# Gate and up pairs with seven products over ten of sixteen k tiles, and tokens kept in DRAM during a half step

## The chip, the cores and the metric

The kernel runs on one core of a Trainium2 chip. The metric is the device time of one execution in microseconds; for comparisons it is the median of several runs. A core has these engines: TensorE (PE in the profile; PEld is its loading of stationary operands), VectorE (DVE), ScalarE (ACT), GpSimd (POOL) and SyncE (SP), and 16 DMA engines. Each engine works through its own instructions in order and waits on semaphores for the others. SP and ACT issue plain DMAs here, POOL also DMAs that add to their destination (accumulating DMAs).

## The reference

A decoder layer over 256 tokens of width 2048, everything in float32. Two half steps, a SwiGLU block each, stand around a mixer and a cross-attention:

```
x = x + 0.5 * swiglu(rms_norm(x, ffn1_norm), ffn1_w_gate, ffn1_w_up, ffn1_w_down)
x = x + hybrid_mixer(rms_norm(x, mix_norm), ...)
x = x + cross_attention(rms_norm(x, xattn_norm), rms_norm(mem, mem_norm), ...)
x = x + 0.5 * swiglu(rms_norm(x, ffn2_norm), ffn2_w_gate, ffn2_w_up, ffn2_w_down)

def swiglu(h, w_gate, w_up, w_down):
    return (jax.nn.silu(h @ w_gate) * (h @ w_up)) @ w_down
```

The hidden width of a half step is 5632, so gate and up are 2048 x 5632 each and down is 5632 x 2048. The mixer and the cross-attention lie between the half steps and are called the middle stage here.

## The kernel before, in words

*Numbers.* A product is taken in a two-part split: each float32 operand is a rounded part "h" and the rest "l" (wh, wl for weights; xTh, xTl and hTh, hTl for tokens and hidden values), and three matmuls, h·h, l·h and h·l, make one product. `wsplit` (line 163, its instructions are `split`, line 160-161) makes wh with a copy on ACT (a "cast") and wl with a subtraction on DVE (a "sub") that reads the raw weights and wh.

*Tiling.* A k tile is 128 rows of a weight matrix; a weight group is 4 k tiles x 512 columns, 1 MB, loaded by one DMA that SP issues (`load`, line 150) into a raw tile. There are 16 k tiles over the model width, and eleven column tiles f over the hidden width. Tokens are two tiles t of 128. A matmul has 512 columns.

*Half step* (`ffn`, line 404). The column tiles are taken in three parts, (0..3), (4..7), (8..10). In a part each f takes a gate/up pair: gate and up products of the tokens, silu of gate (sg, ACT) times up (h, DVE), and a transposition of h (`turn`, lines 408-417) two items later. Then the part's hidden tiles are multiplied by down, in two Strassen groups of two output columns c each; what comes out is added into the tokens `xs` (line 469, DVE), which are kept in SBUF. After the last part `after` makes the next norm, or stores the output.

*Strassen groups* (`strassen`, line 240). The pair of weight columns (left, right) and two k groups (a, b) make seven products instead of eight. This document names them by TensorE's order: P1 (x from the left a weights, ral), P2 (y), P3 (x), P4 (the left b weights, rbl), P5 (x), P6 (the right b weights, rbr), and P7. For P2 and P3 the raw tile ral is added to in place on DVE (lines 255, 273 and 279), each time after the split before has read it; for P5 and P7 accumulating DMAs on POOL's queue add rbr to rar and rbl to ral (line 259). The sums of tokens that P2, P3, P5 and P6 need are made once in a half step (`sums_of`, line 215), and once in a part for h, among P6 of the part's last pair (`mid`); the first is kept in DRAM meanwhile. The k groups that are not in a and b are done plainly (`whole`, line 196), 24 matmuls each, left then right: L0, then P7, then R0, L1, R1. Down's part of three has only L0 and R0. The first pair of a half step is made without seven products (`plain_pair`, line 318).

So in a pair TensorE's order of items is P1 to P6, L0, P7, R0, L1, R1. The transposition of the h of the pair before stands between P2 and P3.

*Slots.* wh and wl have three buffers each (FWB = 3), taken in turn by all items: the split of an item can begin when the item three places ahead has released its slot. Raw tiles have six places in a half step (WRAW + FRAW), taken from a list in a fixed turn (`places`). `in_turn` (line 123) keeps loads, casts and subs each in the order of the program. Otherwise a scheduler orders the instructions of each engine by priority when the program is built; WPRI moves weights' work ahead of the rest.

## Time and profile before

| | |
|---|---|
| median of 3 runs | 1901.0 us (1900.52 to 1901.95) |
| profiled execution | 1900.82 us, span 1898.8 us |
| granted TensorE clock, mean | 0.998 |
| TensorE busy | 1885.3 us, 8616 matmuls |
| DVE, ACT, POOL busy | 1460.8, 1082.2, 123.0 us |
| DMA | 453.90 MB, mean 239 GB/s |

The span goes from the first to the last instruction of one execution. Busy time is the time in which an engine has an instruction under way; matmuls overlap, so that the time from one start to the next is shorter than a matmul's own. In a line of groups stand source line, engine, operation, output and inputs with shapes, the count, busy time in us and mean ns of one, and behind the second bar the idle time of the engine ahead of these instructions, with what ended it. In a timeline stand start and length in us, and in brackets the idle time ahead with its releaser. In a view by stretches stand the stretch, its length, busy time and count for PE, PEld, DVE, ACT and POOL, the granted clock (1.00 is full), the DMA engines' share and GB/s. In the list of DMAs the last number is the median time in us from issue to landing.

### The profile page before, as it was taken

To read this page: it belongs to the slowest core of one execution; us is meant where nothing else is said; L and a number is where in the kernel's file an instruction comes from. 1 tells how busy PE (TensorE), PEld (TensorE's weight loads), DVE (VectorE), ACT (ScalarE), POOL (GpSimd) and SP (SyncE) were. 2 spreads that over 40 slices of the span, in tenths; PEclk is the share of its full clock that TensorE was granted. 3 is DMA by queue.
4 is the path that set the end of the run, shared out by engine and by line. 5 is a ranking of instruction groups with operands and counts; after the bars stand their busy time and mean duration, and the time that the engine had idled before them with its cause. 6 is when DMAs were issued, how large, how long until landed. Compare 5 with 4: busy or idle time off the path is not lost.

```text
span 1898.8 us, 21625 instructions
## 1 busy us (share of the span) xinstructions
PE 1885.3 (99%) x8616; PEld 1561.7 (82%) x8616; DVE 1460.8 (77%) x1174; ACT 1082.2 (57%) x1043; POOL 123.0 (6%) x137
## 2 busy tenths in 40 slices
PE   9999999999999999999999999999999999999998
PEld 7788888888888878778888889888888888888887
DVE  7779887798888975446785565877888878887897
ACT  6556655555555656444576545555655556556663
POOL 2000000000000000002221000000000000000000
PEclk9999999999999999999999999999999999999999
DMA  9876787777777755445465554677768777787775
GB/s 371 294 241 225 244 305 277 274 249 245 269 243 269 260 167 184 157 167 193 170 230 205 190 191 155 245 253 277 232 233 288 262 266 277 256 281 233 241 252 191
DMA packets 68336, 453.90 MB, mean 239 GB/s; under 512 B 7659, under 2 KB 8811, under 8 KB 14860
## 3 DMA queue, kind: packets, MB, share of 16 engines
q1 hardware_dynamic: 56140, 370.74, 49.9%
q0 software_dynamic: 10944, 79.70, 18.7%
q10 hardware_dynamic: 1152, 2.10, 0.3%
q8 instruction: 67, 1.10, 0.2%
q14 instruction: 33, 0.27, 0.0%
HBM read 379.10 MB, written 6.29 MB: 203 GB/s over the span
## 4 chain that ended last, share of the span: by engine, by line
PE 95%; DVE 2%; ACT 1%; issue 1%; DMA 0%; SPq 0%; ACTq 0%; DVEq 0%
PE acc L201 25%; PE x L236 17%; PE acc L193 9%; PE acc L194 9%; PE acc L192 9%; PE acc L236 9%; PE x L201 9%; PE y L236 4%; DVE wl L161 1%; ACT wh L161 1%; PE tp L413 1%; DVE raw L255 1%; DMA raw<-in_ffn_w_up_dram 0%; PE tp L373 0%; PE dsp L690 0%
## 5 line engine op out<-in xcount | busy, mean ns | idle before, releaser
L161 DVE TENSOR_TENSOR wl<-raw,wh 128x2048 fp32r<-128x2048 f32 (+2 forms) x538 | 1014.6, 1905 | 351.8 <-ACT wh L161 351.0
L161 ACT CAST wh<-raw 128x2048 fp32r<-128x2048 f32 (+2 forms) x538 | 853.2, 1600 | 601.3 <-DVE raw L255 180.5
L192 PE MATMUL acc<-wh,xTh 128*128 128x512 f32 x544 | 214.7, 397 | 0.9 <-ACT wh L161 0.8
L193 PE MATMUL acc<-wl,xTh 128*128 128x512 f32 x544 | 212.8, 391 | 0.5 <-DVE wl L161 0.3
L194 PE MATMUL acc<-wh,xTl 128*128 128x512 f32 x544 | 212.5, 391 | 0.0
L255 DVE TENSOR_TENSOR raw<-raw 128x2048 f32<-128x2048 f32 x64 | 146.6, 2291 | 1.9
L259 POOL DMA_DIRECT2D raw<-raw x64 | 55.1, 861 | 1170.4 <-ACT sg L453 478.9
L201 PE MATMUL acc<-wh,xTh 128*128 128x512 f32 x480 | 121.8, 389 | 0.0
L201 PE MATMUL acc<-wl,xTh 128*128 128x512 f32 x480 | 121.8, 389 | 0.0
L201 PE MATMUL acc<-wh,xTl 128*128 128x512 f32 x480 | 121.8, 389 | 0.0
L193 PEld LDWEIGHTS acc<-wl,xTh 128*128 128x128 f32 x544 | 102.6, 189 | 22.9 <-DVE wl L161 2.1
L192 PEld LDWEIGHTS acc<-wh,xTh 128*128 128x128 f32 x544 | 102.4, 189 | 23.0 <-ACT wh L161 1.4
L194 PEld LDWEIGHTS acc<-wh,xTl 128*128 128x128 f32 x544 | 102.5, 188 | 21.5
L201 PEld LDWEIGHTS acc<-wh,xTl 128*128 128x128 f32 x480 | 90.1, 188 | 18.7
L201 PEld LDWEIGHTS acc<-wh,xTh 128*128 128x128 f32 x480 | 90.1, 188 | 18.7
L201 PEld LDWEIGHTS acc<-wl,xTh 128*128 128x128 f32 x480 | 90.1, 188 | 18.7
L236 PE MATMUL x<-wh,sh 128*128 128x512 f32 x256 | 71.8, 403 | 3.1 <-ACT wh L161 3.1
L236 PE MATMUL x<-wh,sl 128*128 128x512 f32 x256 | 69.5, 393 | 0.0
L236 PE MATMUL x<-wl,sh 128*128 128x512 f32 x256 | 69.2, 392 | 0.0
L453 ACT ACTIVATE sg<-acc,r 128x512 f32<-128x512 f32 x24 | 16.5, 690 | 90.1 <-PE acc L201 88.4
L201 PE MATMUL acc<-wl,hTh 128*128 128x512 f32 x232 | 59.3, 390 | 1.8 <-DVE wl L161 1.8
L201 PE MATMUL acc<-wh,hTh 128*128 128x512 f32 x232 | 59.0, 390 | 1.2 <-ACT wh L161 1.2
(339 smaller groups left out, 2827.0 us busy)
## 6 DMA issues: line engine op xcount, KB each, us to landing
raw<-in_ffn_w_down_dram SPq DMA_DIRECT2D x88, 1024.0 KB, 7.5
raw<-in_ffn_w_up_dram SPq DMA_DIRECT2D x87, 1024.0 KB, 8.8
raw<-in_ffn_w_gate_dram SPq DMA_DIRECT2D x86, 1024.0 KB, 8.7
raw<-raw POOLq DMA_DIRECT2D x64, 1024.0 KB, 6.9
raw<-in_w_in_dram SPq DMA_DIRECT2D x48, 1024.0 KB, 4.8
raw<-in_w_out_dram SPq DMA_DIRECT2D x16, 1024.0 KB, 4.8
sl<-ffn_sl POOLq DMA_DIRECT2D x4, 1024.0 KB, 9.0
sh<-ffn_sh POOLq DMA_DIRECT2D x4, 1024.0 KB, 13.0
```

Source lines behind the costliest of these rows:

```text
L161: return SC.copy(wh, src), V.tensor_sub(wl, src, wh.bitcast(F32))
L192: PE.matmul(acc[t], lh, wh, start=first and i == 0, stop=False, skip_group_check=seeded)
L193: PE.matmul(acc[t], lh, wl, start=False, stop=False, skip_group_check=seeded)
L194: PE.matmul(acc[t], ll, wh, start=False, stop=last and i == len(half) - 1, skip_group_check=seeded)
L201: PE.matmul(acc[t], lhs(w[0], t)[i], w[1 + j], start=False, stop=last and j == 1 and n == len(group) - 1, skip_group_check=True)
L236: PE.matmul(acc, lhs(k)[i], w[:, k], start=first, stop=j == 1 and k == 3, skip_group_check=not start)
L255: V.tensor_add(dst, x, y)
L259: G.dma_start(dst, x, accum_op=ALU.add)
L413: PE.transpose(tp[:, j], hs[t][:, j * P:(j + 1) * P], ident)
L453: SC.activation(s, gate[t], AF.Silu, scale=r[:, t:t + 1])
```

## The change: what it does

In a gate/up pair after the first, the seven products now take ten of the sixteen k tiles: a is the k tiles (8, 9, 10, 11, 6), b is (12, 13, 14, 15, 7), five each. The rest is plain: (0, 1, 2, 3) as L0 and R0, 24 matmuls each, and (4, 5) as L1 and R1, 12 each. A product of the pair has 15 matmuls instead of 12. Down's groups stay as they are, with four k tiles.

The tiles wh, wl and raw get room for five k tiles (WK), the raw places of a half step become five (FRAW = 2) and wh and wl keep three buffers. A five-tile load is two DMAs, a five-tile accumulation too (four tiles and one). The sums of tokens get a fifth tile (`more` in `sums_of`), with instructions of their own.

To make room, tokens leave SBUF during a half step: they lie in DRAM tiles `xd`. After the first two parts, what comes out of down is halved by ACT into y (`SC.activation`, four per group) and added to DRAM by an accumulating DMA; in the last part the tokens are loaded into `xc` and added to by DVE as before. At the end of the first half step two of the four token tiles go back to DRAM until the output projection, where SP loads them again; the other two stay. Buffers move between pools: h tiles are six instead of eight, with the fourth hidden tile of a part, the sums' scratch and `xc` in a pool `cp` of two buffers, and the middle stage has 41 instead of 44 small buffers. The stores of the kept sums, and for the first half step a copy of x to DRAM, are issued after the second pair of a half step.

```diff
-UB = 44
+UB = 41
-FRAW = 3
+FRAW = 2
+WK = 5
 FWB = 3
+SEVEN = ((8, 9, 10, 11, 6), (12, 13, 14, 15, 7))
+PLAIN = ((0, 1, 2, 3), (4, 5))
...
+    def CT(shape, dt, name):
+        return cp.tile(shape, dt, tag="c", name=name)
...
+    def wtile(tag, m, n=512):
+        half = phase["half_step"]
+        w = FT(tag, FWB if half else WB, [P, WK if half else 2, 512], F32R, tag)
+        return w.rearrange("p k n -> p (k n)")[:, :m * n].rearrange("p (k n) -> p k n", n=n)
...
-            in_turn("load", SY.dma_start(raw, W[c, g]))
+            raw = raw_tile(place, len(ks), n)
+            kn = W.shape[-2]
+            d = 0
+            while d < len(ks):
+                g, k = divmod(ks[d], kn)
+                m = sum(j // kn == g for j in ks[d:])
+                in_turn("load", SY.dma_start(raw[:, d:d + m], W[c, g, :, k:k + m]))
+                d += m
...
-    def sums_of(ga, gb):
+    def sums_of(ga, gb, more=None):
...
+        if more:
+            f5 = W2([P, 2, S], "f5")
+            V.tensor_add(f5, *(x.bitcast(F32) for x in more))
+            fs.append([f5[:, i:i + 1] for i in range(2)])
...
-                G.dma_start(dst, x, accum_op=ALU.add)
+                for ks in (slice(0, 4), slice(4, len(a))):
+                    if ks.start < len(a):
+                        G.dma_start(dst[:, ks], x[:, ks], accum_op=ALU.add)
...
-                    gate, upv = strassen(wg, f, wu, f, lhs_x, (2, 3), sums, (0, 1),
+                    gate, upv = strassen(wg, f, wu, f, lhs_x, SEVEN, sums, PLAIN,
                                          mid=sums_h if f == part[-1] else None)
...
             for c in range(0, NC, 2):
+                xc = {}
+                if end:
+                    for d in (c, c + 1):
+                        xc[d] = CT([P, TT, 512], F32, "xc")
+                        G.dma_start(xc[d], xd[d])
...
                 for d, acc in zip((c, c + 1), accs):
                     for t in range(TT):
-                        V.scalar_tensor_tensor(xs[d][:, t], acc[t], 0.5, xs[d][:, t], op0=ALU.mult, op1=ALU.add)
+                        if end:
+                            V.scalar_tensor_tensor(xc[d][:, t], acc[t], 0.5, xc[d][:, t], op0=ALU.mult, op1=ALU.add)
+                        else:
+                            with tc.high_priority(WPRI):
+                                y = W2([P, 512], "y")
+                                SC.activation(y, acc[t], AF.Copy, scale=0.5)
+                            G.dma_start(xd[d][:, t], y, accum_op=ALU.add)
...
+    for c in range(2):
+        xs[c] = FT("x", 2, [P, TT, 512], F32, "xs")
+        SY.dma_start(xs[c], xd[c])
...
             norm_chunk(d, xs[d], 64, ss4)
+            G.dma_start(xd[d], xs[d])
```

## The prediction

> **What bounds the kernel now.** I read the page first, then the chain of waits, then the engines' timelines around one gate/up pair.

> ```profile
> span 1898.8 us, 21625 instructions
> PE 1885.3 (99%) x8616; PEld 1561.7 (82%) x8616; DVE 1460.8 (77%) x1174; ACT 1082.2 (57%) x1043; POOL 123.0 (6%) x137
> ...
> PE 95%; DVE 2%; ACT 1%; issue 1%; DMA 0%; SPq 0%; ACTq 0%; DVEq 0%
> ```

> The chain is TensorE for 95% of the span, so a matmul that goes away is time, as long as its weights are there. The chain in order of time gives the price of a product of twelve 512-column matmuls:

> ```profile
> 109.73 2.72 PE acc L236 x12
> ```

> 2.72 / 12 = 0.227 us each. Whether the weights are there is a matter of how far ACT and DVE run ahead, and a view by stretches says how full they are in a plain pair and in the last pair of a part:

> ```profile
> 100.50:142.20 41.70, 41.70 (x189) 34.55 (x188) 32.98 (x20) 23.86 (x17) 1.73 (x2) 1.00 0.73 252
> 139.00:181.00 42.00, 42.00 (x191) 34.77 (x190) 39.23 (x27) 25.94 (x20) 1.73 (x2) 1.00 0.73 245
> ```

> The fourth number is DVE: 32.98 of 41.70 us (79%), and 39.23 of 42 where the sums of h are made too. Not full, but the order matters: splits and additions on the first weights form one serial chain. Here it is for the pair whose P1 starts at 142.21, ACT, DVE and TensorE in turn:

> ```profile
> 129.71 1.91 ACT L161 CAST wh<-raw 128x2048 fp32r<-128x2048 f32 x1 [2.62 <-PE acc L201]
> 136.06 0.69 ACT L453 ACTIVATE sg<-acc,r 128x512 f32<-128x512 f32 x1 [4.43 <-PE acc L201]
> 136.65 1.90 ACT L161 CAST wh<-raw 128x2048 fp32r<-128x2048 f32 x1
> ...
> 143.30 3.72 ACT L161 CAST wh<-raw 128x2048 fp32r<-128x2048 f32 x2 [4.17 <-DVE raw L255]
> ```

> ```profile
> 131.66 2.29 DVE L161 TENSOR_TENSOR wl<-raw,wh 128x2048 fp32r<-128x2048 f32 x1 [2.24 <-ACT wh L161]
> 133.99 2.29 DVE L255 TENSOR_TENSOR raw<-raw 128x2048 f32<-128x2048 f32 x1
> 138.58 2.29 DVE L161 TENSOR_TENSOR wl<-raw,wh 128x2048 fp32r<-128x2048 f32 x1 [2.30 <-ACT wh L161]
> 140.90 2.29 DVE L255 TENSOR_TENSOR raw<-raw 128x2048 f32<-128x2048 f32 x1
> ...
> 145.25 6.70 DVE L161 TENSOR_TENSOR wl<-raw,wh 128x2048 fp32r<-128x2048 f32 x3 [0.74 <-ACT wh L161]
> ```

> ```profile
> 127.70 1.98 PE L201 MATMUL acc<-wh,xTl 128*128 128x512 f32 x8
> 129.51 1.98 PE L201 MATMUL acc<-wl,xTh 128*128 128x512 f32 x8
> ...
> 142.21 1.07 PE L236 MATMUL x<-wh,xTh 128*128 128x512 f32 x4
> ...
> 148.45 1.17 PE L236 MATMUL x<-wh,sh 128*128 128x512 f32 x4
> ```

> The first cast of a pair starts at 129.71, 0.20 us after TensorE has left the wh of R0 of the pair before (129.51). That is the three-buffer rule: item i takes the slot of item i-3, and before P1 stand R0, L1, R1. From there everything is serial: cast, sub, add, cast, sub, add, cast, until 143.30 + 1.91 = 145.21. So the chain is 15.50 us, and TensorE's P1 comes 12.50 us after its start (the lead), P3 6.24 us after P1. P3 has its wh 12.50 + 6.24 - 15.50 = 3.24 us early. That spare is all there is, and the trace has a place where the lead is shorter: the last Strassen group of a part of three hidden tiles, where only L0 and R0 are plain, so that L0, P7 and R0 stand ahead of P1 (ACT, then TensorE):

> ```profile
> 1853.36 1.92 ACT L161 CAST wh<-raw 128x2048 fp32r<-128x2048 f32 x1 [2.62 <-PE x L201]
> ...
> 1867.17 1.91 ACT L161 CAST wh<-raw 128x2048 fp32r<-128x2048 f32 x1 [0.54 <-DVE raw L255]
> ```

> ```profile
> 1863.13 1.07 PE L236 MATMUL x<-wh,hTh 128*128 128x512 f32 x4
> ...
> 1869.12 1.21 PE L236 MATMUL x<-wh,sh 128*128 128x512 f32 x4 [0.39 <-ACT wh L161]
> ```

> The lead is a third of L0, P7 and R0, 1.81 + 2.72 + 5.44 less 0.20 = 9.77 us, as measured; the chain is 15.72, and TensorE waits 0.39 us at P3. So lead plus P1-to-P3 against the chain decides.

> **The change, part by part.** (1) *Matmuls.* Seven products of 15 and plain items of 24, 24, 12, 12 make 177 instead of 180 in each of 20 pairs: 60 x 0.227 = -13.6 us. Nothing else leaves TensorE.

> (2) *The lead.* L1 and R1 have two k tiles now, but each still takes a whole wh/wl slot. Behind R0's wh are left its last third and two items of 2.72 us instead of 5.44: lead 12.50 - 5.44 = 7.06 us.

> (3) *The chain.* Its instructions grow from four tiles to five.

> ```profile
> L161 DVE TENSOR_TENSOR wl<-raw,wh 128x2048 fp32r<-128x2048 f32 x344 | 778.6, 2287 | 211.8 <-ACT wh L161 211.5
> L161 DVE TENSOR_TENSOR wl<-raw,wh 128x1024 fp32r<-128x1024 f32 x190 | 233.2, 1240 | 137.8 <-ACT wh L161 137.4
> ```

> ```profile
> L161 ACT CAST wh<-raw 128x2048 fp32r<-128x2048 f32 x344 | 653.4, 1914 | 434.8 <-DVE raw L255 180.5 <-PE x L201 77.8 <-PE x L236 64.6
> L161 ACT CAST wh<-raw 128x1024 fp32r<-128x1024 f32 x190 | 197.3, 1052 | 165.0 <-PE acc L194 144.6 <-issue 16.1 <-DMA raw<-in_ffn_w_up_dram 1.7
> ```

> A tile more costs (2287 - 1240) / 2 = 0.52 us on DVE and (1914 - 1052) / 2 = 0.43 on ACT; L255 has the length of a sub, so it gets the same. Three casts and four DVE steps: 3.39. The 0.37 us by which sg held the second cast (136.28 to 136.65) go, since gate ends earlier than the chain gets there. Chain 15.50 + 3.39 - 0.37 = 18.52. P1 to P3 grows by six matmuls to 7.60. P3's wh is late by 18.52 - 7.06 - 7.60 = 3.86 us. Then wl: the sub ends 2.85 us after the cast (2.33 now), TensorE wants it ten matmuls (2.27) after P3's start: 0.5 more. So 4.4 us per pair that follows a pair. Those are f = 2, 3, 5, 6, 7, 9, 10, twice: 14 x 4.4 = 61 us. f = 4 and 8 follow a down group with four-tile items; they keep 12.50, and 12.50 + 7.60 covers 18.52: nothing.

> (4) *The first Strassen group of down in each part* also follows a pair; it keeps its chain of four tiles, with the splits of the sums among it (ACT, then TensorE):

> ```profile
> 171.49 1.92 ACT L161 CAST wh<-raw 128x2048 fp32r<-128x2048 f32 x1 [0.37 <-PE acc L201]
> ...
> 186.47 1.91 ACT L161 CAST wh<-raw 128x2048 fp32r<-128x2048 f32 x1 [5.29 <-DVE raw L255]
> ```

> ```profile
> 183.94 1.07 PE L236 MATMUL x<-wh,hTh 128*128 128x512 f32 x4
> ...
> 190.17 1.17 PE L236 MATMUL x<-wh,sh 128*128 128x512 f32 x4
> ```

> Chain 16.89, lead 12.45 - 5.44 = 7.01, P1 to P3 6.23: late by 3.65, and 0.4 for wl. 6 x 4.1 = 24 us. With the sums out of the way (15.50) it would be 2.7 each; with DVE overfull in that pair (39.23 and 2.6 more, against 41.3) up to 6.

> (5) *f = 1 in both halves* follows the plain pair, whose items do not change. The first already waits (row of 62.17 below); its chain grows by 3.39 and its P3 comes 1.36 later, with wl +2.5; I give the second +2. Together 4.5, and the fifth tile's sums (six small DVE instructions, each below the 1.24 us of the 1024-column row) make 0 to 10 the bounds.

> (6) *The clock.* A TensorE that waits can lose its clock. In the first pair of before it does (timeline; then two stretches, PEclk third from the end; then the longer of the two waits in the second stretch):

> ```profile
> 62.17 2.07 PE L236 MATMUL x<-wh,sh 128*128 128x512 f32 x4 [2.69 <-ACT wh L161]
> ```

> ```profile
> 61.50:68.20 6.70, 6.03 (x14) 4.78 (x15) 4.49 (x2) 6.12 (x4) 0.88 (x1) 0.50 0.37 76
> ...
> 683.00:690.00 7.00, 4.98 (x25) 3.90 (x26) 7.00 (x8) 2.48 (x6) 0.00 (x0) 1.00 0.75 214
> ```

> ```profile
> 687.13 0.96 PE L201 MATMUL acc<-wl,hTh 128*128 128x512 f32 x3 [1.80 <-DVE wl L161]
> ```

> After 2.69 us of waiting the granted clock was 0.50 for at least 6.0 us of work, a loss of 3.0 us; after 1.80 it stayed 1.00. The new waits of 3.7 to 3.9 us lie nearer to the first. The half clock also hides the 0.5 us of wl, so a fall costs 2.5. Bounds 0 and 3.0 each; I take half of 2.5, 1.3, because one case does not show that each wait brings it. 20 x 1.3 = 26 us.

> [...]

> (7) *At nothing:* the y copies (ACT, by the sg row 0.69 each, four per down group, ACT is 57% busy) take the place of four DVE additions; their 32 accumulating DMAs, the second piece of each pair's accumulations and the moves of x lie on POOL's queue and the 16 DMA engines (share 0.73 in a pair). Behind a y DMA that waits for ACT stands the next group's second accumulation, which L0 and P7 cover. SP issues twelve loads a pair instead of eight, the middle stage has 41 buffers instead of 44. Cover gone, I put all this at 10 us together; a gain I see nowhere but in DVE's four additions.

> Sum: -13.6 + 61 + 24 + 4.5 + 26 = +102. On the profiled execution's own 1900.8 us (span 1898.8, 2.0 around it; the median is 1901.0, the same) this is 2003 us.

> **The rivals.**
> *The clock hardly falls*, because y's wl takes part of the wait and splits it: 2003 - 26 = 1977 us. For it: 1.80 us left the clock alone.
> *The clock falls at each wait*: 20 x 2.5 = 50 instead of 26: 2027 us. For it: the row of 62.17.
> *The raw tiles come late too.* There are five instead of six, and R0 now loads into rbl's place, which is free once the second accumulation has landed:

> ```profile
> raw<-in_ffn_w_gate_dram SPq DMA_DIRECT2D x86, 1024.0 KB, 8.7
> raw<-raw POOLq DMA_DIRECT2D x64, 1024.0 KB, 6.9
> ```

> Sub of P3 ends at P1 + 14.3; two issues and 6.9 give 22.1, the load 8.7 more, the cast 1.9: 32.7. TensorE wants R0 at 34.5, waits included. 1.8 us spare; landings slower by 4 us would cost 2 us in each of 20 pairs, 2043 us.
> *Faster.* The lead is not lost: if the scheduler places the slots so that the first cast waits for an item before R0, the chain starts earlier. The decision is at a lead of 18.52 - 7.60 = 10.9 us; above it only the 60 matmuls count, 1901 - 13.6 = 1887 us. Against it: in all groups that I followed the first cast starts 0.2 us after R0's wh, whatever stands between, and a slot of two tiles is still a slot.

> **How the numbers follow.** Forecast (1985 to 2018) 0.45; each wait with a clock fall (to 2045) 0.22; hardly any (from 1960) 0.16; raw tiles or POOL late as well (2030 to 2085) 0.10; faster 0.05; the rest, near no change, 0.02. A measurement of this kernel tells 0.2% from no change. Range 1960 to 2045: outside are the faster case, most of the late raw tiles and little else, under 2 in 10. Slower 0.94, within 0.2% 0.01, faster 0.05.

> **What would show it.** Right: 60 matmuls fewer; first cast to P1 7.1 us in a pair after a pair; TensorE idle 3 to 4 us ahead of P3, released by ACT's wh; f = 4 and 8 without it; stretches at clock 0.50 behind some of the waits; a pair every 45 to 48 us. Wrong: leads above 10.9, TensorE busy through P3, DVE idle there, or the long waits released by a DMA.

## The result, and the profile after

The changed kernel takes 2040.5 us (median of 4 runs, 2036.9 to 2047.2) against 1900.8 for the kernel before: ratio 1.074, 95% interval 1.071 to 1.077. The forecast was 2003 us, its range 1960 to 2045. So the sign and the range held, but the likeliest value was 37 us too low, and the result lies 4.5 us below the range's upper end. The profiled execution (2038.4 us) has a span 137.7 us longer than that of before. Its page, the counterparts of the rows shown there, and one group of matmuls:

```profile
span 2036.5 us, 21987 instructions
...
PE 1930.0 (95%) x8556; PEld 1577.5 (77%) x8556; DVE 1506.5 (74%) x1155; ACT 1129.5 (55%) x1077; POOL 197.3 (10%) x227
...
PE 68%; DVE 14%; ACT 8%; DMA 7%; issue 2%; SPq 0%; POOL 0%; ACTq 0%; POOLq 0%; DVEq 0%
...
L274 PE MATMUL x<-wh,sh 128*128 128x512 f32 x296 | 96.2, 459 | 85.8 <-ACT wh L189 68.4
```

TensorE has 60 matmuls fewer and yet 45 us more of busy time, because it worked some of them at half clock (mean clock 0.971, before 0.998). On the chain of waits its share fell from 95 to 68%; ACT, DVE and DMA have come onto it. The last row names the place: the first matmuls of P3 and P5 waited 85.8 us, 68.4 of it for ACT's cast. Here is one of those pairs (its P1 at 335.79) in ACT's and TensorE's timelines:

```profile
328.73 2.34 ACT L189 CAST wh<-raw 128x2560 fp32r<-128x2560 f32 x1 [3.71 <-PE acc L232]
...
336.88 2.34 ACT L189 CAST wh<-raw 128x2560 fp32r<-128x2560 f32 x1 [2.80 <-DVE raw L295]
...
345.03 2.33 ACT L189 CAST wh<-raw 128x2560 fp32r<-128x2560 f32 x1 [0.36 <-DVE raw L295]
```

```profile
335.79 1.29 PE L274 MATMUL x<-wh,xTh 128*128 128x512 f32 x5
...
347.40 1.43 PE L274 MATMUL x<-wh,sh 128*128 128x512 f32 x5 [3.41 <-ACT wh L189]
```

The first cast begins at 328.73 when TensorE lets a slot go, P1 follows 335.79 - 328.73 = 7.06 us later, and the third cast ends at 345.03 + 2.33 = 347.36: a chain of 18.63 us. P3 starts 0.04 us after it, having stood idle for 3.41. The prediction had 7.06, 18.52 and 3.86.

By stretches from one P1 to the next (the clock stands third from the end), three pairs that follow a pair, and a part's first down group:

```profile
335.80:380.90 45.10, 41.69 (x186) 33.97 (x185) 36.82 (x21) 25.31 (x17) 3.49 (x4) 1.00 0.75 235
380.90:427.60 46.70, 43.29 (x187) 35.11 (x185) 39.69 (x25) 25.50 (x17) 3.49 (x4) 0.96 0.77 246
427.60:475.30 47.70, 44.29 (x187) 35.89 (x185) 38.17 (x23) 27.31 (x20) 3.49 (x4) 0.93 0.68 210
...
202.20:246.80 44.60, 42.33 (x189) 34.47 (x188) 36.41 (x21) 25.88 (x19) 4.34 (x5) 1.00 0.78 253
```

All three pairs had the same wait. They differ in the clock: none, 3.41 or 6.83 us at half speed, which makes 45.1, 46.7 or 47.7 us where before had 41.7. With the starts of all P1 in both traces the 137.7 us are placed as follows (the forecast's terms, matmuls and clock included, beside them):

| place | count | forecast, us | measured, us |
|---|---|---|---|
| before the first P1 | 1 | 0 | +7.1 |
| f = 1 | 2 | +3.1 | +0.9 |
| pairs that follow a pair | 14 | +70.3 (5.0 each) | +73.6 (5.3 each) |
| first down group of a part | 6 | +32.4 (5.4 each) | +17.7 (2.95 each) |
| pairs after a down group (f = 4, 8) | 4 | -2.7 | +27.7 (6.7 to 7.1 each) |
| middle stage, second down groups | | 0 | +3.7 |
| last down group and end | 1 | 0 | +7.1 |

So the largest term was right to 5%, one was nearly twice too large, and some 45 us stand in places that the forecast had put at nothing. The largest of these, f = 4:

```profile
280.96 2.34 ACT L189 CAST wh<-raw 128x2560 fp32r<-128x2560 f32 x1 [4.27 <-DMA raw<-in_ffn_w_gate_dram]
```

```profile
300.11 2.50 PE L274 MATMUL x<-wh,sh 128*128 128x512 f32 x5 [4.33 <-ACT acc L314]
```

P1 is at 287.87, so the lead is 6.9 us and not 12.5; what held the first cast was no slot but the load of the left raw tile. P3 then waited 4.33 us, the last 0.5 of it for the copy of c0l, which stood behind the third cast on ACT, and went on at half clock (2.50 us for five matmuls).

### The profile page after: what moved, and what is told of

The parts are those of the page before. It is cut to its first block, busy times and chain, and to the rows that moved or that the text cites. A ratio compares the mean times of both kernels' runs of the same rounds, so it can differ in the third digit from the quotient of the medians.

```text
span 2036.5 us, 21987 instructions
## 1 busy us (share of the span) xinstructions
PE 1930.0 (95%) x8556; PEld 1577.5 (77%) x8556; DVE 1506.5 (74%) x1155; ACT 1129.5 (55%) x1077; POOL 197.3 (10%) x227
## 4 chain that ended last, share of the span: by engine, by line
PE 68%; DVE 14%; ACT 8%; DMA 7%; issue 2%; SPq 0%; POOL 0%; ACTq 0%; POOLq 0%; DVEq 0%
PE x L274 15%; PE acc L232 11%; PE acc L224 8%; PE acc L274 8%; PE acc L225 8%; PE acc L223 8%; ACT wh L189 8%; DVE wl L189 7%; DVE raw L295 6%; PE x L232 4%; DMA raw<-in_ffn_w_gate_dram 4%; PE y L274 1%; DMA raw<-in_ffn_w_down_dram 1%; DMA raw<-raw 1%; DMA x<-xc 0%
## 5 line engine op out<-in xcount | busy, mean ns | idle before, releaser
L189 DVE TENSOR_TENSOR wl<-raw,wh 128x1024 fp32r<-128x1024 f32 (+3 forms) x538 | 1047.8, 1967 | 417.7 <-ACT wh L189 398.8
L189 ACT CAST wh<-raw 128x1024 fp32r<-128x1024 f32 (+3 forms) x538 | 874.7, 1646 | 656.9 <-PE acc L225 142.8
L223 PE MATMUL acc<-wh,xTh 128*128 128x512 f32 x544 | 216.2, 400 | 7.5 <-ACT wh L189 7.5
L224 PE MATMUL acc<-wl,xTh 128*128 128x512 f32 x544 | 214.7, 395 | 1.2 <-DVE wl L189 1.2
L225 PE MATMUL acc<-wh,xTl 128*128 128x512 f32 x544 | 214.6, 394 | 0.0
L301 POOL DMA_DIRECT2D raw<-raw x104 | 90.8, 990 | 1071.8 <-DVE raw L295 694.3
L274 PE MATMUL x<-wh,sh 128*128 128x512 f32 x296 | 96.2, 459 | 85.8 <-ACT wh L189 68.4
L295 DVE TENSOR_TENSOR raw<-raw 128x2560 f32<-128x2560 f32 (+1 forms) x64 | 168.0, 2624 | 2.0
L274 PEld LDWEIGHTS x<-wh,sh 128*128 128x128 f32 x296 | 61.5, 217 | 105.6 <-ACT wh L189 74.3
L232 PE MATMUL acc<-wh,xTl 128*128 128x512 f32 x360 | 94.6, 389 | 0.0
L232 PE MATMUL acc<-wl,xTh 128*128 128x512 f32 x360 | 94.6, 389 | 0.0
L232 PE MATMUL acc<-wh,xTh 128*128 128x512 f32 x360 | 94.6, 389 | 0.0
L274 PEld LDWEIGHTS x<-wh,sl 128*128 128x128 f32 x296 | 67.0, 226 | 16.4
L274 PEld LDWEIGHTS x<-wl,sh 128*128 128x128 f32 x296 | 57.8, 196 | 13.6 <-DVE wl L189 0.7
## 6 DMA issues: line engine op xcount, KB each, us to landing
raw<-in_ffn_w_down_dram SPq DMA_DIRECT2D x88, 1024.0 KB, 7.7
raw<-in_ffn_w_up_dram SPq DMA_DIRECT2D x67, 1024.0 KB, 7.7
raw<-in_ffn_w_gate_dram SPq DMA_DIRECT2D x66, 1024.0 KB, 9.7
raw<-raw POOLq DMA_DIRECT2D x64, 1024.0 KB, 6.9
raw<-in_w_in_dram SPq DMA_DIRECT2D x48, 1024.0 KB, 4.8
raw<-in_w_out_dram SPq DMA_DIRECT2D x16, 1024.0 KB, 4.8
raw<-in_ffn_w_gate_dram SPq DMA_DIRECT2D x44, 256.0 KB, 10.1
```

Of the source, the lines that this page charges most:

```text
L189: return SC.copy(wh, src), V.tensor_sub(wl, src, wh.bitcast(F32))
L223: PE.matmul(acc[t], lh, wh, start=first and i == 0, stop=False, skip_group_check=seeded)
L224: PE.matmul(acc[t], lh, wl, start=False, stop=False, skip_group_check=seeded)
L225: PE.matmul(acc[t], ll, wh, start=False, stop=last and i == len(half) - 1, skip_group_check=seeded)
L232: PE.matmul(acc[t], lhs(w[0], t)[i], w[1 + j], start=False, stop=last and j == 1 and n == len(group) - 1, skip_group_check=True)
L274: PE.matmul(acc, lhs(k)[i], w[k][j], start=first, stop=j == 1 and k == len(w) - 1, skip_group_check=not start)
```

## The experiments

The theory to be tested: P3 is late because cast, subtraction, add, cast, subtraction, add, cast stand in one chain behind a first cast that the slots release 7 us ahead of P1. Rivals: the raw tiles' places; DVE as a whole; for f = 4 and 8, the new token DMAs, the reload of the sums, or the places.

### The short plain groups first

```diff
-PLAIN = ((0, 1, 2, 3), (4, 5))
+PLAIN = ((4, 5), (0, 1, 2, 3))
```

> The changed kernel with the two plain groups of a pair exchanged: k tiles (4, 5) are L0 and R0, (0, 1, 2, 3) are L1 and R1. Same work, same sizes on every engine. Theory A, the lead (two short items ahead of P1 cost the chain its start): first cast to P1 is 12.5 us again in the 14 pairs that follow a pair and in the first down groups, P3 does not wait there and the clock does not fall there; 14 pairs at 41.0 instead of 46.5 us on average and 6 groups 2.9 shorter: 2040 - 100 = about 1940 us. f = 4 and 8 stay at 47 to 48 us. Rival B, DVE is full with five-tile work: the work is the same, so within 10 us of 2040. Rival C, raw tiles are late: R0 is wanted 2.7 us earlier, so a wait for a DMA stands ahead of R0 and the time stays at 2040 or rises.

1995.9 us (ratio 1.050, 1.049 to 1.052): faster than after by 45 us, but far from 1940. The leads of the pairs grew to 8.6 to 11.6 us, the chain itself to 19.6 to 20.1, and then something else held the first cast (ACT's timeline; P1 at 370.51):

```profile
360.90 2.34 ACT L189 CAST wh<-raw 128x2560 fp32r<-128x2560 f32 x1 [1.70 <-DMA raw<-in_ffn_w_gate_dram]
```

SP issues its loads in order, and one of them waits for rbl's place until the second accumulation has landed, at 347.7, 21.5 us after P1. The four loads behind it then come in one burst, the next pair's left tile last (360.80). The pairs that follow a pair are at +43.2 us in place of +73.6. So the slots decide at 4/2, and behind them, some 1.5 to 4.5 us further on, the raw places decide.

### Three and three

```diff
-PLAIN = ((0, 1, 2, 3), (4, 5))
+PLAIN = ((0, 1, 2), (3, 4, 5))
```

> The changed kernel with plain groups of three k tiles each, (0, 1, 2) and (3, 4, 5). Theory A: lead 1.36 + 4.08 + 4.08 - 0.20 = 9.3 us, so P3 is late by 18.6 - 9.3 - 7.6 = 1.7 us and 0.3 more for wl, instead of 3.5 and 0.5; the clock falls rarely, as after the 1.80 us of before. 14 x 2 less wait, some 26 less for the clock, first down groups without a wait (15.5 against 9.3 + 6.2), 18 less: 1965 to 1980 us. Rival B (DVE full) or C (raw tiles): no such step, 2030 to 2050.

1992.8 us (1.049, 1.047 to 1.051). The stretch of a pair, and its P3:

```profile
327.50:371.40 43.90, 41.90 (x186) 33.91 (x185) 36.84 (x21) 25.26 (x18) 3.47 (x6) 1.00 0.79 247
```

```profile
336.87 1.43 PE L274 MATMUL x<-wh,sh 128*128 128x512 f32 x5 [1.51 <-ACT wh L189]
```

The 14 pairs go from +73.6 to +34.2 us and the first down groups from +17.7 to +10.1; f = 4 and 8 stay (+26.1) and the start stays (+7.9), as the expectation's sum had left them. The run is 13 us above the upper end of what was expected, since the pairs gained 39 us where 54 had been worked out, and the first down groups 8 where it was 18. One k tile moved from one plain group to the other, with all else in place, makes the lead 9.32 us instead of 7.05, and P3 starts 9.35 us after P1 instead of 11.62: what the lead gains, P3 gains. The wait shown at P3 falls from 3.41 to 1.51 us.

### The gap filled

Fifteen matmuls whose result nobody reads, between the transpositions and P3 in each pair:

```diff
+            for i in range(15):
+                in_turn("fill", PE.matmul(fl, hi[:, 0, 0:P], ..., start=i == 0, stop=i == 14))
         product(x, s_(1), parts(ral), False)
```

> The changed kernel with 15 more matmuls between the transposition and P3 of each seven-product pair, on data that is there, into a PSUM tile that nobody reads: 3.4 us of TensorE work in the place of the 3.5 us wait. If the half clock comes from the waiting (theory), it does not fall in these pairs: the chain still sets P3, a pair after a pair takes 45.1 us instead of 46.7 or 47.7, and the sum falls by 26 us for the 14 pairs and about 10 for f = 4 and 8: about 2005 us, with f = 1 of the second half, which waits only 0.8, longer by up to 3. Rival (the clock does not matter to the end, as the chain and not TensorE sets the next start): no change, 2040.

2017.5 us (1.062, 1.060 to 1.064). A pair, and the fill:

```profile
330.40:375.70 45.30, 45.06 (x202) 36.78 (x201) 36.85 (x21) 25.32 (x17) 3.49 (x4) 1.00 0.76 240
```

```profile
338.84 3.69 PE L325 MATMUL fl<-xTh 128*128 128x512 f32 x15 [0.24 <-ACT ys L329]
...
342.37 1.30 PE L274 MATMUL x<-wh,sh 128*128 128x512 f32 x5
```

P3 starts 11.99 us after P1, 0.4 later than in after, but all 14 pairs now take 45.3 us, none longer, and together they are at +50.4 instead of +73.6. With P3 held as long and the idleness gone the falls of the clock are gone (1.00 in this pair; 0.994 over the run, 0.971 in after): in after they cost at least these 23.2 us, 1.7 a pair. The rival of no change is out, but the run is 12 us above what was expected: f = 4 and 8 gained 1.9 us in place of 10, and where little waited the fill only adds (f = 1 of the second half is at +6.0 instead of +0.7).

### The kernel before with five raw places

```diff
-FRAW = 3
+FRAW = 2
```

> The kernel before with five raw places in a half step instead of six, nothing else. Theory R (too few raw places make the loads after the second accumulation of a down group one burst, which delays the first cast of f = 4 and 8 by 5 us): those four pairs start their first cast at a lead of 7 to 9 us instead of 12.5, P3 waits 1 to 3 us there, and the last group of the program too: 1905 to 1925 us. Rival (the DMAs of the tokens and the larger sums of the change do it): first cast of f = 4 and 8 as before, 1899 to 1903 us.

1907.0 us (1.004, 1.003 to 1.006). The pairs that follow a pair do not move, so the sixth place explains nothing there. f = 4 and 8 lose 0.7 to 1.6 us each, 4.5 of the 27.7. The direction is right (P1 at 263.73, lead 11.6 instead of 12.5; ACT's timeline):

```profile
252.15 1.91 ACT L161 CAST wh<-raw 128x2048 fp32r<-128x2048 f32 x1 [3.03 <-DMA raw<-in_ffn_w_gate_dram]
```

### Without the DMAs that add the parts

```diff
                             with tc.high_priority(WPRI):
                                 y = W2([P, 512], "y")
                                 SC.activation(y, acc[t], AF.Copy, scale=0.5)
-                            G.dma_start(xd[d][:, t], y, accum_op=ALU.add)
```

> The kernel after without the 32 accumulating DMAs that add the first two parts' down outputs to the tokens in DRAM (the ACT copies of y stay; the output lacks those two parts). It looks at the four pairs that follow a down group (f=4 and f=8 in both halves), whose periods grew by 6.7 to 7.1 us each, 27.7 in sum, because the left raw tile of the pair landed at 280.86, 18 us after its issue. Theory Y: these DMAs, with their stretch of 181 GB/s, push the down group's second accumulation and the loads behind it back; without them the four periods fall to about +2 each, the time to about 2020. Theory S: the burst that follows the accumulation is too much by itself (three down loads, the pair's tiles and 2.5 MB of the first sums): the four periods stay at +6 to +7, the time at 2035 to 2041.

One run: 2036.5 us. The four periods are at +7.2, +7.0, +6.6 and +4.8. The stretch after P1 of the second down group, here and in after:

```profile
247.70:261.50 13.80, 13.80 (x62) 11.31 (x61) 11.77 (x7) 10.86 (x8) 0.86 (x1) 1.00 0.47 96
```

```profile
246.80:260.70 13.90, 13.90 (x62) 11.22 (x62) 11.87 (x7) 10.85 (x8) 2.59 (x3) 1.00 0.94 172
260.70:281.00 20.30, 20.30 (x91) 16.83 (x90) 10.84 (x6) 7.69 (x5) 1.12 (x2) 1.00 0.93 370
```

Half of what the DMA engines did there is gone (share 0.94 to 0.47), but the first cast of f = 4 still waits for its load, with a lead of 6.8. 25.6 of the 27.7 us stay, so these DMAs are not the main cause. What follows in after is the third row: 20 us at 370 GB/s, 7.5 MB in one burst once the second accumulation has landed.

### The reload of the sums behind the raw tiles, and the token copies later

```diff
-                    for x, d in zip(hsums[-1], kept):
-                        G.dma_start(x.bitcast(F32), d)
+                for x, d in zip(new, kept):          # called by strassen behind load(ral), load(rar)
+                    in_turn("load", SY.dma_start(x.bitcast(F32), d))
...
-                        G.dma_start(d, x.bitcast(F32))
+                        in_turn("copy", G.dma_start(d, x.bitcast(F32)))
...
-                            G.dma_start(xd[c], A["x"][0, ...])
+                            in_turn("copy", G.dma_start(xd[c], A["x"][0, ...]))
```

> The kernel after with two moves. The reload of the token sums (2.5 MB, twice per half) goes onto SP's queue behind the next pair's left and right raw tiles, where it stood on POOL's queue ahead of them; and the copies of the tokens in DRAM wait for the stores of the sums, where they were issued at 1.3 us. The two are read apart by their places: start and the four pairs after a down group. Start, both theories: first P1 7 us earlier, since the copies took the first weights' bandwidth. Theory S (the reload ahead of the pair's left tile made it late): it lands about 6.5 us earlier, the four periods fall from +6.9 to about +3 and less, the time to 2013 to 2020. Theory Y (the DMAs of y, or the raw places, make it late): the four periods stay above +6, only the start is gained, 2033.

2020.6 us (1.063, 1.061 to 1.065). The comment in the diff is not in the kernel. The two moves act in different places; the copies now go out at 46.6 to 48.3 us.

*Start.* In after three of the four copies of the tokens, emitted behind the second pair, waited for nothing and were issued at 1.3 to 3.0 us, beside the first weights (list of DMAs from 0 to 16 us, and TensorE's timeline):

```profile
x<-in_x_dram POOLq DMA_DIRECT2D x3, 512.0 KB, 10.2
```

```profile
15.73 1.22 PE L223 MATMUL acc<-wh,xTh 128*128 128x512 f32 x2 [2.66 <-ACT wh L189]
```

The first P1 came at 59.63, here at 54.14, before at 52.54: 5.5 of the 7.1 us are the copies.

*f = 4 and 8.* +4.5, +4.0, +4.6 and +4.3 instead of 6.7 to 7.1. The first cast now waits for its slot, and with P1 at 282.57 its lead is 12.49, as before the change:

```profile
270.08 2.34 ACT L189 CAST wh<-raw 128x2560 fp32r<-128x2560 f32 x1 [2.62 <-PE acc L232]
```

With this lead P3 waits 0.7 us at f = 4, for the copy of c0l, and not at all at f = 8. What is left is the end of the same burst: in this pair rbl's second load lands at 293.75, and P4, which follows, waits 2.2 us; at f = 8 P5 waits 2.7 to 3.0 us. The granted clock over the f = 4 pair (282.57 to 327.88) was 0.96. So the periods fell a little less than expected. The reload, 2.5 MB ahead of the pair's own tiles, took 10.3 of the 27.7 us, and what remains shows at the next tiles in the queue.

### Without the second add

```diff
-        add(ral, ral, rbr)
         product(x, s_(1), parts(ral), False)
```

> The kernel after without the second add of each seven (left raw tile += second right tile; 32 adds left out, so the third and seventh products use a sum that lacks one of its three tiles). The third split then needs no add and can follow the second cast directly: from the start of the first cast to the end of the third some 13 us where it was 18.6. Theory A (P3 is late because cast, subtraction, add, cast, subtraction, add, cast stand in one chain behind a late first cast): no wait at P3 in the 14 pairs and the six first down groups, no clock falls there; each pair +5.3 to between 0 and +1 (60 to 74 less), the first down groups +2.95 to 0 (18 less), the four pairs after a down group and the last group some 4 to 6 less each: 1920 to 1945. Rival (DVE as a whole is short of time, not the chain: it is busy for some 36 of a pair's 42 us): the wait moves to a later product and more than half of the pairs' loss stays: 1970 to 2010.

1945.3 us (1.024, 1.021 to 1.027), 95 us less than after. The stretch of a pair, ACT's second and third cast, and P3:

```profile
360.70:402.10 41.40, 41.40 (x186) 33.96 (x185) 36.44 (x24) 25.07 (x17) 3.49 (x4) 1.00 0.85 267
```

```profile
361.80 4.58 ACT L189 CAST wh<-raw 128x2560 fp32r<-128x2560 f32 x2 [2.80 <-DVE raw L295]
```

```profile
368.68 1.41 PE L274 MATMUL x<-wh,sh 128*128 128x512 f32 x5
```

The third cast follows the second directly, and P3 has its weights 2.3 us early. All 14 pairs take 41.4 us, 0.3 less than before: together -4.4 instead of +73.6. The first cast still starts 7.05 us ahead of P1, the slots and places are those of after, and DVE is busy 36.44 of 41.40 us, a larger share than in after (36.82 of 45.10). The rival that DVE is short as a whole falls; it is the order of seven steps. The last group, too, is at -0.7 us instead of +7.1.

Two expectations were not met. The first down groups stayed at +2.0 to +4.0 and f = 4 and 8 at +7.7 to +8.9, with a new releaser (TensorE's timeline of a first down group):

```profile
199.92 1.16 PE L274 MATMUL x<-wh,sh 128*128 128x512 f32 x4 [1.88 <-DVE acc L323]
```

That is P5, which may add to x only when DVE has made c0r from it, and this subtraction stands on DVE behind a split and two of a turn's subtractions.

### The fourth product early

If the chain is too long for what lies between P1 and P3, then P4, which needs no add, could be put there:

```diff
+        early = parts(rbl)
+        third = parts(ral)
+        product(c0l, of(b, 0), early, False)
-        product(x, s_(1), parts(ral), False)
+        product(x, s_(1), third, False)
         with tc.high_priority(WPRI):
             V.tensor_sub(c0r, ys, x)
-        product(c0l, of(b, 0), parts(rbl), False)
         accumulate(ral, rbl)
```

> The kernel after with the fourth product (c0l, from the right-hand k tiles' left raw tile) and its split moved ahead of the third in every seven. TensorE then has 3.4 us more work before P3, and the split of rbl falls into ACT's and DVE's gaps beside the adds. Theory A (P3 is late because of the chain of three splits behind a late first cast): P3's wait of 3.5 us goes down to 0 to 0.5, no clock falls are left in the 14 pairs; each pair +5.3 to about +0.6 (66), the six first down groups +2.95 to about 0 (17), the pairs after a down group and the last group lose 3.4 and a clock fall each (15 to 20): 1935 to 1945. Rival (ACT and DVE have no room: the moved split takes its 2.4 and 2.7 us out of the chain itself): P3's wait stays at 2 to 3.5 us, 2005 to 2040.

2065.5 us (1.087, 1.085 to 1.089): slower than after. DVE, then TensorE (P1 at 339.45):

```profile
342.92 5.56 DVE L189 TENSOR_TENSOR wl<-raw,wh 128x2560 fp32r<-128x2560 f32 x2 [1.14 <-ACT wh L189]
348.40 0.68 DVE L377 TENSOR_TENSOR hTl<-tp,hTh 128x512 fp32r<-128x512 f32 x1
349.00 2.82 DVE L295 TENSOR_TENSOR raw<-raw 128x2560 f32<-128x2560 f32 x1
...
359.74 0.69 DVE L327 TENSOR_TENSOR acc<-ys,x 128x512 f32<-128x512 f32 x1
```

```profile
354.28 1.43 PE L274 MATMUL x<-wh,sh 128*128 128x512 f32 x5 [3.17 <-ACT wh L189]
...
360.57 1.40 PE L274 MATMUL x<-wh,sh 128*128 128x512 f32 x5 [2.00 <-ACT wh L189]
```

The scheduler put the moved subtraction and one of a turn between the second subtraction and the second add, so the chain grew by what P4 had given. And a second wait came, of 1 to 2 us ahead of P5. P5 may add to x only when DVE has made c0r from it. In after P4 stands between P3 and P5 and covers this; here nothing does, and the subtraction, behind two splits on DVE, ends at 360.43, 0.14 us before P5 starts. The row names ACT's cast instead, the fourth in a row, which ends at 360.50; but in the first down groups and in f = 4 and 8 that cast ends after P5 has started, and P5 follows the subtraction by 0.14 to 0.15 us all the same. In some pairs one matmul of L0 is placed between P3 and P5 and does wait for that cast, to about the same time. Neither expectation was met.

The second try held the adds to their turn among DVE's subtractions:

```diff
-                V.tensor_add(dst, x, y)
+                in_turn("sub", V.tensor_add(dst, x, y))
...
         add(ral, ral, rar)
+        early = parts(rbl)
         accumulate(rar, rbr)
         product(y, s_(0), parts(ral), True)
```

> The fourth product early as in the first try, but with the adds held to their turn on DVE: first subtraction, first add, subtraction of the moved split, second subtraction, second add. In the first try the moved split's subtraction and two turn copies stood between the second subtraction and the second add. Theory A: the moved split's subtraction still takes about 2 us of DVE between the first add and the second subtraction, so the chain grows from 18.6 to about 20.4 while P3 is due 3.4 later: its wait falls from 3.5 to about 2.0 to 2.4, which costs no clock; pairs +2.4 to +3, first down groups about +1: 1985 to 2000. Rival (DVE has no room for any other order; what P3 gains, P5 and the plain tiles lose): 2025 to 2065, as the first try.

2102.1 us (1.106, 1.103 to 1.110). P3's wait did fall to 0.7 us, but the second wait stayed:

```profile
364.63 1.42 PE L274 MATMUL x<-wh,sh 128*128 128x512 f32 x5 [0.68 <-ACT wh L189]
...
370.90 0.80 PE L232 MATMUL acc<-wh,xTh 128*128 128x512 f32 x1 [2.00 <-ACT wh L189]
```

In this pair it is the matmul of L0 that waits for its cast; the subtraction for c0r ends at 370.77, so without this matmul P5 would have waited almost as long. The clock fell there (0.96 from 355.18 to 402.50), and after a down group P2's cast now stands on ACT behind the cast of the last-loaded tile (waits of 8.2 to 9.3 us at P2). Neither expectation was right.

### Put together

Three and three, the reload behind, the copies late and the fourth product early in its first form; then the same without the fourth product but with the third part's token loads behind the group's second accumulation; then that with the fourth product in turn:

```diff
-PLAIN = ((0, 1, 2, 3), (4, 5))
+PLAIN = ((0, 1, 2), (3, 4, 5))
...
-                        G.dma_start(xc[d], xd[d])
+                        in_turn("queue", G.dma_start(xc[d], xd[d]))    # called behind accumulate(ral, rbl)
```

> The kernel after with the fourth product early, plain groups of three and three k tiles, the reload of the sums behind the next pair's raw tiles and the copies of the tokens behind the stores of the sums. Theory A: with the early fourth product the chain needs a lead of about 15.2 - 6.8 = 7 to 8 us, and three plus three gives 9.3: no wait is left at P3 in the pairs and the first down groups, and the start costs nothing. What remains is a late left tile after a down group (0 to 3 each) and the last group (3 to 4), against 13.6 us of matmuls fewer: 1887 to 1905. Rival (the raw tiles' places decide once the slots do not): the loads that wait for the second accumulation, 21 us after P1, come too late for the pairs, about 2 us each: 1915 to 1940.

> The kernel after with plain groups of three and three k tiles, the reload of the sums behind the next pair's left and right raw tiles, the copies of the tokens behind the stores of the sums, and in the third part the loads of the tokens behind the group's second accumulation. The product order is unchanged. If the parts add up: 1992.8 (three and three) less 6 at the start, less 2.5 for each of the four pairs after a down group, less 2 for the last group: 1973 to 1977. If the reload on SP's queue holds up the loads behind it, which wait there until the down group's last product has read the old sums: 1985 to 2000. Neither reaches 1900, since P3's wait of 1.65 per pair stays.

> The same with the fourth product early and in turn. P3 is due at first cast + 9.3 + 11.0 and ready at about first cast + 21: wait 1 or less, pairs +1 to +1.5 where three and three alone had +2.2. Against that the moved product needs the last loaded raw tile of the four earlier, which landed late after a down group when this was tried with the other order. Theory A: 1955 to 1975. Rival (late raw tiles after a down group take the gain): 1980 to 2005, above the kernel without the move.

2027.6 us (1.068, 1.066 to 1.069), 1976.8 (1.040, 1.037 to 1.043) and 2118.4 (1.115, 1.110 to 1.120). The second is as its parts add up: start +1.6, pairs +41.5, first down groups +10.1, f = 4 and 8 +12.7. It is the best of the variants that do the whole computation, and no match for the kernel before. Its pairs are 7 us worse than with three and three alone, since some of them now wait 2 to 3 us at P3; the cause stays open. The token loads, moved, changed nothing that can be told: the last group is at +6.2.

The first and third met neither of their expectations. They lose by the early fourth product, with the second wait behind P3 in every pair that follows a pair (1.5 to 2.0 us; one matmul of L0 waits for its cast, and the subtraction for c0r ends within 0.4 us of that cast), and in the third P2's cast behind that of the last-loaded tile.

## Why the prediction was right, and where not

*(1) Matmuls* and *(2) the lead*: as measured, 60 fewer, 7.05 us.

*(3) The chain*: 18.62 measured for 18.52, P3 idle 3.40 to 3.42 for 3.86. That this chain is the cause is shown from both ends: a longer lead takes the wait down (three and three), a shorter chain takes it away. A pair without a fall costs +3.4; the sum 4.4 - 0.7 had said 3.7.

*(3), f = 4 and 8 "nothing"*: the step that failed, and with it the sign "f = 4 and 8 without it": P3 waited 4.3 us there. "They keep 12.50" was true of the slots, and when the raw tile came in time the lead was 12.49. The step left out the load: the reload of the sums, grown to 2.5 MB, and five-tile loads with one place fewer stand in one burst after the second accumulation. The rival of late raw tiles named this mechanism but placed it at R0 in each of 20 pairs; there it did not occur. Shown: places alone 4.5 us (in the kernel before), reload 10.3; the DMAs that add the parts, 2.1 at most. How the rest divides stays open.

*(4) First down group*: over-sized. The wait was 2.09 us for 3.65 and brought no fall of the clock in any of the six. The chain measured 15.53, not 16.89: the splits of the sums, which stood among it before, no longer do. The "2.7 each" that the prediction gave for the sums out of the way was near: 2.95.

*(5)* was 2.2 us too high.

*(6) The clock*: 1.3 a wait was near the mark in sum by luck. In the 14 pairs falls cost 1.7 each by the filled kernel; in the six down groups nothing. Half of 2.5 was no mean over chances there: 12 of the 14 pairs fell, the six shorter waits not.

*(7) At nothing*: 10 us were allowed, outside the sum, and 17.9 came. The start's 7.1 had no place in the working: the copies of x were read where the program has them, behind the second pair, but nothing tied them there. The middle stage's 3.7 stay open. In the last group (7.1) the step that failed is the one of f = 4 and 8: the first cast waited for its load, so the lead was 7.00 us where it had been 9.77, and P3 waited 3.59 where it had waited 0.39 (ACT, then TensorE; P1 at 1993.81):

```profile
1986.81 1.91 ACT L189 CAST wh<-raw 128x2048 fp32r<-128x2048 f32 x1 [1.92 <-DMA raw<-in_ffn_w_down_dram]
```

```profile
2003.03 1.20 PE L274 MATMUL x<-wh,sh 128*128 128x512 f32 x4 [3.59 <-ACT wh L189]
```

Later in the group R0 was late as well and waited 1.83 us, to 2025.21, with the clock at half from there for 3.41 us; on POOL's queue the second accumulation stood behind a token load that waited for the output:

```profile
2006.97 0.56 POOL L520 DMA_DIRECT2D xc<-x  x1 [7.12 <-DMA out_dram<-xc]
2007.52 0.92 POOL L301 DMA_DIRECT2D raw<-raw  x1
```

That this queue is a cost of its own is not shown. With the token loads where they are and the second add out, the group is at -0.7 us; with the token loads moved, in the combined kernel, P3 still waits 3.11 us and the group is at +6.2.

So (4) gave 15 us too much, and f = 4 and 8, the start, the middle and the end 48 too little; that is nearly all of the 37 us. The result fell among the values given to a fall of the clock at each wait (to 2045), but that is not what happened, and that errors of both signs left it just inside the range is in part luck.

## What to carry to other kernels

When work is regrouped, look for the longest serial chain through several engines and subtract it from the time between the event that lets it start and the work that needs it; a saving of 0.7 us a pair was lost eight times over because both ends moved. A term put at nothing because "its slots do not change" needs the same reading of its loads, with the bytes that stand ahead of them in the same burst. A transfer without a dependency is issued when the scheduler likes (three copies of x at 1.3 to 3.0 us here), and a product moved by hand changes the planned order of its neighbours and uncovers what it had covered (the wait of 1 to 2 us ahead of P5 here).

## What the runs showed of the hardware

By length alone the same waits look like chance. Of the waits of over 1.2 us behind the first 40 us of the two profiles, 0 of 2 below 1.6 us had a fall that began between the wait's start and 3.42 us after its end, 1 of 2 of 1.6 to 2.0, 2 of 8 of 2.0 to 2.8, 13 of 16 of 2.8 to 3.6, and all 4 longer ones (4.32 to 4.34); of the 14 waits of 3.40 to 3.42 us in the pairs that follow a pair, 12 had one.

*With accumulating DMAs the engines were as busy at half the rate.* In the rows under the fifth experiment the DMA engines were busy to 0.94 at 172 GB/s in the stretch in which POOL's queue with accumulating DMAs had 769 of the 770 packets, and to 0.93 at 370 GB/s in the loads after it. The packets of the first stretch were also smaller (3.1 KB against 7.1 on average), and no run tells the two causes apart.
